# Two thousand columns of an expert's down matrix, moved from the ring into the memory of x

## The chip, the core and the metric

The kernel runs as one program on one core of a Trainium2 chip. The metric is device time in microseconds of one execution; 1854.32 us is the median of three executions of the kernel before (1853.71 to 1855.75).

## What is computed

Two blocks of two layers each work on x, 256 tokens of 1024 numbers, held transposed as eight tiles of 128 x 256. The first block has three kinds of attention and a gated feed-forward part. A layer of the second block, where the change lies, is, cut short:

```
def hybrid_layer(x, ...):
    hn = rms_norm(x, norm_mix)
    ...                                   # attention, latent attention, short convolution
    x = x + einsum('bsc,cd->bsd', mixed, w_out)
    x = x + expert_choice_moe(rms_norm(x, norm_ffn), w_router, b_router, w_gate, w_up, w_down)

def expert_choice_moe(x, ...):            # 16 experts, each takes its 32 best tokens
    gate, idx = lax.top_k(softmax(logits).transpose(0, 2, 1), cap)
    xs = x[bidx, idx]
    hid = silu(xs @ w_gate) * (xs @ w_up)
    return zeros_like(x).at[bidx, idx].add((hid @ w_down) * gate)
```

Each expert has three matrices of 1024 x 1024 fp32 (gate, up, down), 4 MB each. They are read once, so a layer's 16 experts bring 201 MB from HBM.

## The kernel before

**The ring.** All weights stand in HBM as one long stream in the order of use (`ring_plan`, L493). The kernel reads it through a ring in SBUF, 128 partitions x 36096 columns (`RING`, L27; 1024 columns are 512 KB). `layout` (L553) gives each piece a place, one behind the other, and starts again at 0 when a piece doesn't fit. A chunk is one matrix of 8192 columns; `wanted` (L535) says into which pieces it is cut. A piece can be loaded once the instructions that read the older data in the same columns are done.

**Places beside the ring.** Expert 1 (`SPARE`, L31) of each second-block layer gets some pieces elsewhere, written as negative numbers in `wanted`: of its up matrix 2048 columns go into the tile `cst`, six times 512 into the buffers `whi` and `wlo`, four times 256 into `rows_c` and `kb` tiles; of its down matrix eight times 256 go into `kb` tiles. The rest of the down matrix, 2048 and 4096 columns, lies in the ring. `fetch` (L838) makes the tiles and the DMAs.

**The stage around the change.** When x of a layer is complete (x8, eight views of the tile `xT`), the router normalizes it and finds each expert's tokens: a short chain of small steps, with four rounds of `max` and `match_replace` on VectorE (L1731). Meanwhile sixteen transposes bring the normalized x into token order (L1755, four PSUM banks), and eight matmuls with the identity lay x into four PSUM banks, `yj` (L1726); onto these the experts add their outputs, and at the end of the stage x8 is written back from `yj` (L1829). Between these two points nothing reads x8. `gather(0)` (L1768) makes the inputs of experts 0 to 7 with 32 matmuls and eight copies; then expert 0's gate matmuls begin (L1788).

**The order.** No engine runs in program order: `Program.order` (L447) plans all instructions of the whole kernel at once. It schedules forward and backward in turn, `ROUNDS` times, each round ranked by the times of the one before; it keeps the round that its own model finds shortest. The first rank is shaken by random numbers, one seed for each of the four layers (`SEEDS`, L145; entry 2 is the first layer of the second block). An instruction that needs a PSUM bank may be taken early only where the buffers that lie between it and the oldest unissued instruction leave one free (`held`, L368). All DMAs go to SyncE's queue (SP) in the planned order, and a DMA that waits holds up those behind it.

Of the kernel before, what the change touches and what calls it, by code (L numbers as in the profile page):

```python
# [17 lines left out]
T = 256  # L18
# [8 lines left out]
RING, WIDEST = 36096, 4096  # L27
# [107 lines left out]
class Program:  # L135
# [5 lines left out]
    WINDOW, SLACK, MIX = 4000, 0.0, 0.2  # L141
    IN_ORDER = ("whi", "wlo")
    TICK, BUSY = 3413.0, 3060.0
    ROUNDS, PREFER, WAIT = 7, 3000.0, 1.0
    SEEDS, SHAKE = (20, 16, 1, 1), 20.0  # L145
    SWITCH, OTHER = 95.0, {"V": "S", "S": "V"}

    def __init__(self):
# [386 lines left out]
def wanted(tag):  # L535


    kind = tag[0]
    if kind == "early":
        return 2048, 1024, 1024  # L540
    if kind == "eu" and tag[2] == SPARE:
        return (2048, -2048) + (-512,) * 6 + (-256,) * 4
    if kind == "ed" and tag[2] == SPARE:
        return (-256,) * 8 + (2048, WIDEST)
    if kind in ("eg", "eu", "ed") and GATHER < tag[2] < NE - 1:
        return (2 * WIDEST,)
    if kind == "ed" and tag[2] == NE - 1:
        return 4096, 2048, 1024, 1024
    return (WIDEST,)


def layout():

    at, out = 0, []
    for tag in ring_plan():
        cuts, done, pieces, want = cuts_of(tag), 0, [], list(wanted(tag))
        while done < cuts[-1]:
            w = want.pop(0) if len(want) > 1 else want[0]
            if w < 0:
                pieces.append((-w, None))  # L560
                done -= w
                continue
            fits = [c for c in cuts if done < c <= done + min(w, RING - at)]
            if not fits:
                at = 0
                want.insert(0, w)
                continue
            pieces.append((fits[-1] - done, at))
            at += fits[-1] - done
            if fits[-1] - done < min(w, cuts[-1] - done):  # L570
                want.insert(0, w - (fits[-1] - done) if w - (fits[-1] - done) >= 1024 else w)
            done = fits[-1]
        out.append((tag, pieces))
    return out
# [211 lines left out]
def hybrid_kernel(ctx: ExitStack, tc: tile.TileContext, A, out, taps=None):  # L786
    nc = tc.nc
    prog = Program()
    V, S, PE, DMA = (Engine(prog, k, e) for k, e in
                     (("V", nc.vector), ("S", nc.scalar), ("PE", nc.tensor), ("D", nc.sync)))  # L790

    ringp = ctx.enter_context(tc.tile_pool(name="ringp", bufs=1))
    res = ctx.enter_context(tc.tile_pool(name="res", bufs=1))
# [6 lines left out]
    def nm(s):  # L800
        uid[0] += 1
        return f"{s}_{uid[0]}"

    def kb(dt=F32):
        return prog.tile(res, [128, 256], dt, nm("kb"), "kb", 26)
# [6 lines left out]
    def one_of(pool, shape, name, dt=F32):  # L812
        return prog.tile(pool, shape, dt, nm(name), name, 1)
# [8 lines left out]
    ring = ringp.tile([128, RING], F32, name="ring")  # L822
    lying = []

    ahead = []

    def prefetch(others={}):
        tag, pieces = plan[state["at"]]
        ahead.append((tag, fetch(pieces, others)))

    def chunk(*tag):
        if not ahead:
            prefetch()
        got, t = ahead.pop(0)
        assert got == tag, (got, tag)
        return t

    def fetch(pieces, others):  # L838
        state["at"] += 1
        cols, tiles, spare = [0], [], 0  # L840
        for i, (n, at) in enumerate(pieces):
            o = state["off"]
            state["off"] += 128 * n
            before = []
            if at is not None:
                t = View(Slot(lambda at=at, n=n: ring[:, at:at + n], None), [128, n], F32)
                before = [v for a, b, v in lying if a < at + n and b > at]
                lying[:] = [(a, b, v) for a, b, v in lying if not (a >= at and b <= at + n)]
                lying.append((at, at + n, t))
            elif n == 2048:  # L850
                t = one_of(res, [128, 2304], "cst")
            elif n == 512:
                spare += 1
                t = prog.tile(wk, [128, 512], F32, nm("spare"), ("whi", "wlo")[spare % 2], 3)
            elif pieces[i - 1][0] == 512:
                t = one_of(res, [128, 256], "rows_c")
            else:
                t = kb()
            DMA.dma_start(t[:, :n], A["ring"][o:o + 128 * n].rearrange("(p f) -> p f", p=128), after=before)
            for dst, src in others.get(i, ()):  # L860
                DMA.dma_start(dst, src)
            cols.append(cols[-1] + n)
            tiles.append(t)
        return Chunk(cols, tiles)
# [6 lines left out]
    xT = one_of(res, [128, 8, T], "x")  # L871
    x8 = [View(Part(xT, (slice(None), k)), [128, T], F32) for k in range(8)]
# [4 lines left out]
    cst = one_of(res, [128, 2304], "cst")  # L877
# [5 lines left out]
    for q in range(4):  # L883
        prefetch()
        prefetch({0: [(ck, A["ck"]), (cf, A["cf"])]} if q == 2 else {0: [(pv, A["pv"]), (dl, A["dl"])]} if q == 3 else {})
# [179 lines left out]
    for k0, k1, dst in ((0, 4, rows_c[0][:, :512]), (4, 6, rows_c[0][:, 512:]), (6, 8, rows_c[1])):  # L1065
        p = tps()
# [794 lines left out]
```

## Time and profile before

| | |
|---|---|
| median of 3 | 1854.32 us |
| the profiled execution | 1855.18 us |
| its span, first to last instruction | 1853.4 us |
| TensorE matmuls busy | 1485.4 us (80%) |
| VectorE, ScalarE busy | 800.0 us, 649.4 us |
| read from HBM | 591.66 MB |
| granted TensorE clock, mean | 0.903 of full speed |

The 1.8 us between span and time lie outside the instructions. The page's busy time of TensorE is no bound by itself: the stages have different limits, so the page is read by stretches of time, then the waits of a stretch. The two expert stages lie at about 836 to 1265 us and 1419 to 1848 us, the mixers of the second block ahead of each. TensorE's clock has two levels here, granted 1.00 (2.4 GHz) and 0.50 (1.2 GHz).

### The profile page before, as it was taken

What the parts mean: (1) busy time and instruction counts of PE and PEld (TensorE: products, weight loads), DVE (VectorE), ACT (ScalarE), POOL (GpSimd) and SP (SyncE); (2) the same over time, 40 slices, a digit from 0 to 9 for tenths busy, and PEclk for the clock granted to TensorE, in tenths of its full rate; (3) what the DMA queues carried; (4) which work ended last, traced back from release to release, by engine and by line L of the source; (5) the groups of instructions that cost most, each with busy time, mean ns of one, the idle gap of its engine ahead of it and who ended that gap; (6) DMA issues with size and microseconds to landing.
All of it is one profiled execution on the core that took longest, in us unless ns stands there. A gap on an engine that the chain in (4) does not pass through costs nothing.

```text
span 1853.4 us, 34566 instructions
## 1 busy us (share of the span) xinstructions
PE 1485.4 (80%) x14566; PEld 1180.7 (64%) x14566; DVE 800.0 (43%) x2141; ACT 649.4 (35%) x1588; POOL 0.2 (0%) x4
## 2 busy tenths in 40 slices
PE   7999999999999999988566565668998756555655
PEld 6888999888899998875333233337786433333332
DVE  4997769789776786780000000004684000000000
ACT  3865545468554565742000000005762100000001
POOL 0000000000000000000000000000000000000000
PEclk9999999999999999999788878788998888777777
DMA  9979555664454542449999999999456999999997
GB/s 392 426 323 423 209 177 213 254 277 179 167 216 172 199 169 92 165 168 389 429 429 429 430 430 431 429 426 425 165 204 241 431 429 431 430 431 428 430 431 324
DMA packets 44362, 594.93 MB, mean 321 GB/s; under 512 B 5040, under 2 KB 8752, under 8 KB 15536
## 3 DMA queue, kind: packets, MB, share of 16 engines
q1 hardware_dynamic: 44208, 592.73, 77.7%
q8 instruction: 114, 1.87, 0.4%
q14 instruction: 40, 0.33, 0.0%
HBM read 591.66 MB, written 1.05 MB: 320 GB/s over the span
## 4 chain that ended last, share of the span: by engine, by line
PE 51%; DMA 39%; DVE 7%; ACT 1%; issue 1%; SPq 0%; DVEq 0%; ACTq 0%
PE ps L485 41%; DMA ring<-in_ring_dram 39%; PE ps L481 10%; DVE kb L485 3%; ACT kb L485 1%; DVE wlo L485 1%; DVE ring L485 1%; DVE ti L485 1%; DVE h L485 0%; ACT whi L485 0%; DVE x L485 0%; DVE whi L485 0%; SPq L485 0%; DVE aff L485 0%; ACT ti L485 0%
## 5 line engine op out<-in xcount | busy, mean ns | idle before, releaser
L481 PE MATMUL ps<-ring,kb 128*32 128x256 f32 x6016 | 463.2, 475 | 277.1 <-DMA ring<-in_ring_dram 273.3
L481 PEld LDWEIGHTS ps<-ring,kb 128*32 128x32 f32 x6016 | 241.9, 135 | 487.2 <-issue 248.1
L485 PE MATMUL ps<-h,whi 128*128 128x256 f32 x2944 | 436.6, 288 | 9.5 <-DVE h L485 7.6
L485 PEld LDWEIGHTS ps<-h,whi 128*128 128x128 f32 x2944 | 391.7, 194 | 14.6 <-DVE h L485 8.2
L485 DVE TENSOR_TENSOR wlo<-ring,whi 128x512 fp32r<-128x512 f32 (+1 forms) x512 | 335.8, 676 | 96.3 <-ACT whi L485 60.3
L485 DVE TENSOR_TENSOR kb<-kb,ps 128x256 f32<-128x256 f32 x76 | 31.8, 420 | 791.6 <-ACT kb L485 791.3
L485 ACT CAST whi<-ring 128x512 fp32r<-128x512 f32 (+1 forms) x441 | 267.1, 610 | 239.5 <-PE ps L485 212.0
L485 ACT ACTIVATE kb<-ps 32x256 f32<-32x256 f32 (+3 forms) x178 | 66.4, 378 | 571.0 <-PE ps L481 554.3
L485 PE MATMUL ps<-h,wlo 128*128 128x256 f32 x1472 | 247.1, 285 | 0.0
L485 PEld LDWEIGHTS ps<-h,wlo 128*128 128x128 f32 x1472 | 208.8, 193 | 0.3
L485 ACT COPY kb<-ps 128x256 f32<-128x256 f32 (+2 forms) x234 | 78.4, 364 | 287.6 <-PE ps L481 212.4
L485 PE MATMUL ps<-cm,kb 128*128 128x128 f32 (+2 forms) x554 | 85.3, 276 | 49.0 <-DVE kb L485 46.3
L485 PEld LDWEIGHTS ps<-cm,kb 128*128 128x128 f32 (+1 forms) x554 | 68.3, 166 | 74.9 <-DVE kb L485 50.3
L481 PE MATMUL ps<-kb,kb 32*128 32x256 f32 (+6 forms) x1036 | 98.6, 376 | 12.2 <-ACT kb L485 10.1
L485 PE MATMUL ps<-kb,whi 128*128 128x256 f32 x704 | 99.5, 279 | 0.5 <-DVE kb L485 0.4
L481 PEld LDWEIGHTS ps<-kb,kb 32*128 32x128 f32 (+4 forms) x1036 | 67.1, 171 | 36.5 <-ACT kb L485 20.9
L485 PEld LDWEIGHTS ps<-kb,whi 128*128 128x128 f32 x704 | 89.6, 188 | 0.9 <-DVE kb L485 0.9
L485 ACT ACTIVATE kb<-kb,ti 128x256 f32<-128x256 f32 (+1 forms) x161 | 71.2, 462 | 10.8 <-DVE ti L485 10.4
L485 PE MATMUL ps<-kb,wlo 128*128 128x256 f32 x352 | 58.1, 279 | 0.0
L485 DVE TENSOR_TENSOR kb<-kb,kb 128x256 f32<-128x256 f32 (+2 forms) x135 | 55.9, 422 | 3.5 <-ACT kb L485 1.9
L485 PE MATMUL ps<-whi,h 128*128 128x512 f32 (+1 forms) x192 | 55.3, 377 | 0.0
L485 DVE SCALAR_TENSOR_TENSOR kb<-ps,pv,kb 128x255 f32<-128x255 f32 (+2 forms) x102 | 48.3, 480 | 12.5 <-ACT kb L485 11.3
(171 smaller groups left out, 1028.3 us busy)
## 6 DMA issues: line engine op xcount, KB each, us to landing
ring<-in_ring_dram SPq DMA_DIRECT2D x58, 4096.0 KB, 35.1
ring<-in_ring_dram SPq DMA_DIRECT2D x97, 2048.0 KB, 12.2
ring<-in_ring_dram SPq DMA_DIRECT2D x27, 1024.0 KB, 12.4
ring<-in_ring_dram SPq DMA_DIRECT2D x13, 1536.0 KB, 26.3
ring<-in_ring_dram SPq DMA_DIRECT2D x10, 1920.0 KB, 7.7
ring<-in_ring_dram SPq DMA_DIRECT2D x4, 3584.0 KB, 35.4
ring<-in_ring_dram SPq DMA_DIRECT2D x27, 512.0 KB, 16.2
ring<-in_ring_dram SPq DMA_DIRECT2D x4, 3072.0 KB, 36.8
```

The source lines that it names most:

```text
L481: call(*[self.real(a) for a in args], **{k: self.real(v) for k, v in kw.items()})
L485: o.call(*[self.real(a) for a in o.args], **{k: self.real(v) for k, v in o.kw.items()})
```

## The change

The down matrix of expert 1 keeps its eight pieces in `kb` tiles and its last 4096 columns in the ring. Its middle 2048 columns no longer lie in the ring: one DMA of 1024 KB brings them into the tile `xT`, and the chunk's columns of that part are the eight views x8. Because the tile is x's own, this DMA follows the last reader of x8, among them the eight identity matmuls. Each second-block layer then takes 2048 columns less of the ring, and what follows in the ring lies 2048 columns further ahead. Two settings of the planner change with it: six rounds in place of seven, and seed 6 in place of 1 for the first layer of the second block.

```diff
-    ROUNDS, PREFER, WAIT = 7, 3000.0, 1.0
-    SEEDS, SHAKE = (20, 16, 1, 1), 20.0
+    ROUNDS, PREFER, WAIT = 6, 3000.0, 1.0
+    SEEDS, SHAKE = (20, 16, 6, 1), 20.0
@@ def wanted(tag):
     if kind == "ed" and tag[2] == SPARE:
-        return (-256,) * 8 + (2048, WIDEST)
+        return (-256,) * 8 + (-2048, WIDEST)
@@ def prefetch(others={}):
-        ahead.append((tag, fetch(pieces, others)))
+        ahead.append((tag, fetch(tag, pieces, others)))
@@ def fetch(tag, pieces, others):
             elif n == 2048:
-                t = one_of(res, [128, 2304], "cst")
+                t = one_of(res, [128, 2304], "cst") if tag[0] == "eu" else None
 ...
+            if at is None and n == 2048 and tag[0] == "ed":
+                DMA.dma_start(xT, A["ring"][o:o + 128 * n].rearrange("(p k t) -> p k t", p=128, t=T), writes=x8)
+                cols += [cols[-1] + T * (k + 1) for k in range(8)]
+                tiles += x8
+                continue
```

## Rows read from the trace of the kernel before

**Rows 1.** The page, span in 40 slices of 46 us: busy tenths, clock, DMA
```profile
PE   7999999999999999988566565668998756555655
PEclk9999999999999999999788878788998888777777
DMA  9979555664454542449999999999456999999997
GB/s 392 426 323 423 209 177 213 254 277 179 167 216 172 199 169 92 165 168 389 429 429 429 430 430 431 429 426 425 165 204 241 431 429 431 430 431 428 430 431 324
```
**Rows 2.** The chain that ended last: start us, us, what
```profile
836.23 14.02 PE ps L481 x256
...
878.68 38.37 DMA ring<-in_ring_dram
...
1222.90 34.03 DMA ring<-in_ring_dram
...
1419.17 14.02 PE ps L481 x256
...
1819.95 24.56 DMA ring<-in_ring_dram
```
**Rows 3.** Windows: stretch, length, busy us of PE, PEld, DVE, ACT, POOL; clock, DMA share, GB/s
```profile
700.00:725.00 25.00, 23.85 (x180) 21.55 (x178) 16.56 (x33) 13.58 (x31) 0.00 (x0) 1.00 0.30 120
1100.00:1200.00 100.00, 59.10 (x704) 30.45 (x704) 2.72 (x8) 4.91 (x15) 0.00 (x0) 0.78 1.01 431
1350.00:1375.00 25.00, 23.78 (x185) 21.83 (x184) 22.22 (x60) 17.69 (x52) 0.00 (x0) 1.00 0.68 269
```
**Rows 4.** Timeline of SP, the issues before each expert stage: start us, us, issue
```profile
817.64 2.35 SPq L485 DMA_DIRECT2D spare<-in_ring_dram  x5
836.92 3.73 SPq L485 DMA_DIRECT2D ring<-in_ring_dram  x3
...
1399.04 2.73 SPq L485 DMA_DIRECT2D spare<-in_ring_dram  x4
1419.78 20.28 SPq L485 DMA_DIRECT2D ring<-in_ring_dram  x8
```
**Rows 5.** Windows of one and two us around each stage's start (columns as rows 3)
```profile
824.00:826.00 2.00, 0.10 (x1) 0.00 (x0) 1.81 (x7) 1.10 (x4) 0.00 (x0) 1.00 1.05 404
828.00:830.00 2.00, 1.40 (x6) 1.21 (x6) 1.84 (x6) 0.00 (x0) 0.00 (x0) 0.50 0.00 0
836.00:837.00 1.00, 1.00 (x19) 0.58 (x21) 0.42 (x1) 0.98 (x3) 0.00 (x0) 1.00 0.00 0
839.00:840.00 1.00, 1.00 (x24) 0.65 (x20) 0.00 (x0) 0.00 (x0) 0.00 (x0) 1.00 0.97 410
1414.00:1416.00 2.00, 2.00 (x12) 2.00 (x11) 1.89 (x7) 0.75 (x2) 0.00 (x0) 0.50 0.00 0
```
**Rows 6.** Timeline of TensorE across the router: idle before it and releaser in brackets
```profile
820.97 1.94 PE L485 MATMUL ps<-cm,kb 128*128 128x128 f32 x16
823.71 0.39 PE L485 MATMUL ps<-cm,aff 128*16 128x128 f32 x2 [0.80 <-DVE aff L485]
828.09 0.36 PE L485 MATMUL ps<-cm,kb 16*128 16x16 f32 x2 [3.99 <-DVE kb L485]
828.74 0.63 PE L485 MATMUL ps<-sel,ck 128*128 128x32 f32 x2 [0.28 <-DVE sel L485]
830.51 5.73 PE L485 MATMUL ps<-kb,h 128*128 128x256 f32 x32 [0.74 <-DVE kb L485]
836.16 11.43 PE L481 MATMUL ps<-ring,kb 128*32 128x256 f32 x208
...
1412.82 6.35 PE L485 MATMUL ps<-kb,h 128*128 128x256 f32 x32 [0.74 <-DVE kb L485]
```
**Rows 7.** Timeline of TensorE: identity matmuls on x (two records each), projection matmuls
```profile
880.86 1.76 PE L485 MATMUL ps<-x,cm 128*128 128x256 f32 x4
...
905.26 1.03 PE L485 MATMUL ps<-x,cm 128*128 128x256 f32 x4
...
800.78 1.25 PE L485 MATMUL ps<-h,whi 128*128 128x256 f32 x9
```
**Rows 8.** Timeline of VectorE: last write of x, last round, readers of the transposes
```profile
818.04 0.42 DVE L485 TENSOR_TENSOR x<-ps,x 128x256 f32<-128x256 f32 x1
...
827.87 0.46 DVE L485 SCALAR_TENSOR_TENSOR h<-ps,ti,h 128x256 fp32r<-128x256 f32 x1
...
830.71 1.26 DVE L485 SCALAR_TENSOR_TENSOR h<-ps,ti,h 128x256 fp32r<-128x256 f32 x3
```
**Rows 9.** DMA issues: to, from, count, KB each, us from issue to landing
```profile
ring<-in_ring_dram SPq DMA_DIRECT2D x1, 1024.0 KB, 5.1
x<-in_x_dram SPq DMA_DIRECT2D x1, 1024.0 KB, 5.2
```

More of the change, by code (lines that the diff above doesn't have):

```diff
@@ L836, in chunk, with fetch @@
         return t
-    def fetch(pieces, others):
+    def fetch(tag, pieces, others):
         state["at"] += 1
```

## Prediction

> **What bounds the kernel now.** I read the 40 slices first [rows 1]. They split the span in two kinds of stretch. In the mixers TensorE is at 9 tenths and the DMA engines idle half the time; in the two expert stages it is the other way round, the DMA engines at 9 and about 430 GB/s, TensorE at 5 to 6. The windows say the same sharper: 1100 to 1200 us has DMA share 1.01 and 431 GB/s with TensorE busy 59 of 100 us, while 700 to 725 us has TensorE busy 23.85 of 25 us and DMA share 0.30 [rows 3]. The chain of waits agrees: from 836 us to the end it is a burst of TensorE, then DMA pieces of 25 to 38 us joined by short TensorE pieces [rows 2]. So an expert stage ends when its bytes have come: its length is (bytes not yet on chip when the stream becomes saturated) / 430 GB/s, and its end moves with the moment of saturation and with what was loaded before it. Fuller buffers in mid-stage are worth nothing, since the DMA engines never rest there.
>
> The moment of saturation is seen in three views. SP issues its last DMA before the stage at 817.64 us, five in 2.35 us, and the next at 836.92 us [rows 4]. Between them the DMA engines finish what was queued and then stand still: share 1.05 at 824 to 826, 0.00 at 828 to 830 and at 836 to 837, 0.97 from 839 us [rows 5]. TensorE's first expert matmul is at 836.16 us [rows 6], so the issue at 836.92 us is a piece that waited for ring columns which expert 0's gate matmuls read. The second layer repeats it: last spare issues at 1399.04 us, next ring issue 1419.78 us, share 0.00 before it [rows 4, 5]. There are thus some 8 us of idle DMA ahead of each stage, with the ring full. That is what the change can use.
>
> **The change, part by part.**
>
> *The DMA into x.* One DMA of 1024 KB is removed from the ring and one of the same size is added, so no bytes and no issues are added. If it runs in the idle 8 us, the stage has 1.049 MB less to bring: 1.049 MB / 430 GB/s = 2.44 us. The DMA must start after the identity matmuls and land before the stream starts again. Alone, such a DMA lands 5.1 to 5.2 us after its issue [rows 9]; issued by about 831 us it is clear of a restart at 836 to 838 us. If it overlaps the restart a little, its bytes are still moved early, as the engines are not saturated before 839 us.
>
> The Trainium skill states, in "DMA: Bandwidth & Descriptors", Specifications, that HBM gives one core about 358 GB/s. By that the megabyte would be worth 2.93 us. The trace's 430 GB/s disagrees, and decides.
>
> *A later restart.* Ring arithmetic, first layer: expert 0's gate matrix lies at columns 6144 to 14336, and the removed piece at 5120 to 7168. It waited only for the first of the eight groups of gate matmuls (1024 columns each): 836.92 - 836.16 = 0.76 us. After the change the first ring DMA of the stage is the 4096-column piece, now at 5120 to 9216; it must wait for three groups. 208 records in 11.43 us are 0.055 us each [rows 6], a group has eight, so two more groups are 0.88 us. In the second layer everything lies 2048 columns lower, gate 24832 to 33024 and the piece 23552 to 27648: three groups again, against one before. So each layer gains 2.44 - 0.88 = 1.56 us, both 3.1 us, if TensorE's times stay.
>
> *The identity matmuls.* Before, they run deep in the expert stage, at 880.86 us and later, in gaps, where they cost nothing [rows 7]. Now a DMA waits for them, so the planner has a reason to put them ahead of the stage. x is complete at about 818.5 us [rows 8]. A pair of them takes 1.03 us at the full clock (905.26 us) and 1.76 us where most of it ran at the low one (880.86 us) [rows 7]; four pairs make 4.1 to 7.0 us. What can cover that: TensorE's idle stretches in the router, 0.80 + 3.99 + 0.28 + 0.74 = 5.8 us, of which 3.99 us is one piece, while VectorE does the four rounds [rows 6]. In that piece all the matmuls fit at the full clock, nearly. The limit is PSUM: sixteen transposes fill four of eight banks at 820.97 us [rows 6], and VectorE reads the last of them only at 827.87 to 831.97 us [rows 8]. With the router's own bank, three of the four banks for x are free in the gap, so six matmuls (3.1 us) fit there and the last two (1.0 us) fall into the smaller gaps up to 830.5 us. Then nothing on the path is delayed, and the DMA can issue at about 831 us. If the cover is gone, each pair pushes gather and expert 0 back by its 1.03 to 1.76 us.
>
> *The clock.* After the long idle piece the granted clock is 0.50 (1.2 GHz) at 828 to 830 us, and TensorE starts gather in it; the second layer has 0.50 at 1414 to 1416 us [rows 5]. Gather's 32 matmuls take 5.73 and 6.35 us [rows 6]. Matmuls of the same shape at 1.00 are spaced (1.25 - 0.28) / 8 = 0.12 us, taking 0.28 us as the length of one record [rows 7], so 32 of them take about 4.0 us. If the identity matmuls fill the gap and the clock stays at 2.4 GHz, gather ends up to 1.7 and 2.3 us sooner, and the restart with it: 0 to 4.0 us in sum. I take half, 2.0 us, because two of the gaps remain and the eight copies between gather's matmuls may bind first.
>
> *Planner settings.* Seed and round count change no work, but the whole order. In the mixers TensorE idles 1.2 us of 25 (700 to 725, 1350 to 1375 us) [rows 3], so there is little to win or lose in a stage; I take 0 and plus or minus 2 us as an estimate from these two rows. The eight views in place of one, and the write of x8 at the stage's end long after, cost nothing: same matmuls, same columns.
>
> *Sum.* 3.1 + 2.0 = 5.1 us, between 3.1 and 7.1. The profiled execution, 1853.4 us of span in 1855.18 us, would become 1850.1; it lies 0.9 us above the median of the three, so on the median 1854.32 - 5.1 = 1849.2 us, between 1847.2 and 1851.2 without the reordering.
>
> **The rivals.**
>
> *Identity matmuls on the path (slower).* The planner ranks them by the backward pass, where the DMA into x comes just before the first ring piece of the stage; that puts them near gather or between gather and expert 0. There each microsecond of them delays expert 0, and so the restart. All eight cost 4.1 to 7.0 us; with the 0.88 us and less the 2.44 us that is 2.5 to 5.4 us for a layer, 5.1 to 10.9 for both: 1859.4 to 1865.2 us. It decides from 1.56 us of such work per layer, about a pair. For it: PSUM is crowded there [rows 6, 8], and before, the planner left the 3.99 us empty although x was ready. Against it: before, it had no reason to hurry.
>
> *The DMA into x comes too late to matter.* Should the identity matmuls stay behind the start of expert 0, the DMA joins a saturated stream and gains nothing; the later restart is left, 2 x 0.88 us: 1856.1 us. The change then does not do what it says. For it: they stood at 880.86 us before [rows 7]. Against it: SP's order is planned too, and the DMA's place in the stream is early.
> The Trainium skill, "DMA: Bandwidth & Descriptors", Anatomy of one DMA, says that DMA engines don't wait on semaphores; the issuing sequencer waits before dispatch. So a late DMA into x, if placed early on SP, would hold the ring pieces behind it. What this would do here: each microsecond that x's readers end after about 837.8 us delays the restart by as much, so a pair of identity matmuls behind expert 0's first groups adds 1.0 to 1.8 us per layer, 1858 to 1860 us; no row shows such a hold on SP in the gap, and I count it in this rival with 0.04.
>
> *Reordering outweighs it.* If the new order of the four layers is worth more than 2 us either way, 1846 to 1858 us without any help from the change. For it: all stages are planned anew. Against it: the small idle shares [rows 3].
>
> **How the numbers follow.** Forecast 0.55; too late 0.15 (with the 0.04); on the path 0.17; reordering 0.13. Less than 0.2% (3.7 us) is about what a measurement of this kernel can tell from no change; faster means below 1850.6 us. The forecast, with its 2 us of reordering, lies below that in four of five parts: 0.43, and 0.05 from reordering: 0.48. Within 0.2%: the rest of the forecast 0.12, most of "too late" 0.11, partly covered matmuls 0.06, reordering 0.04: 0.33. Slower: 0.19. The range runs from 1847.2 less 2 us of reordering, 1845, to 1856.1 plus 2, 1858; it leaves out the bulk of "on the path" and the ends of reordering, some 0.2.
>
> **What would show it.** In the timeline of TensorE, identity matmuls between 818 and 831 us and gather starting no later than 830.5 us; the granted clock there 1.00 or 0.50. On SP, a DMA into x at about 831 us and the first ring issue some 0.9 us behind the third gate group. In the windows, a DMA share above zero between 828 and 836 us. Each stage's length from expert 0's first matmul to x8's write-back should fall by about 1.6 us, the rest lies ahead of it. Wrong would be: identity matmuls next to gather with expert 0 later by more than 1.6 us, or the DMA into x behind the first ring piece, or a difference that stands in the first 800 us.

## The result: 10.8 us slower, in the mixers

The changed kernel takes 1865.82 us (median of 4, 1864.78 to 1870.17) against 1855.03 us for the kernel before: a ratio of 1.006, 95% interval 1.0048 to 1.0072. The forecast was 1849.2 us and the range ended at 1858; the sign and the range were both wrong. The profiled execution has a span of 1863.6 us in 1865.53 us, 10.2 us more than before. One profiled execution further below, that of the first held run, took 3463.09 us against 1851.03 to 1856.02 us of its ten others; no stage time is taken from it.

The page of the changed kernel, the lines that answer to [rows 1], 40 slices of 46.6 us:

```profile
PE   7999999899999999989566555558999765655655
PEclk9999999999999999989878788888999877878788
DMA  9989555665454541448999999999346999999997
```

The picture is the same: mixers bound by TensorE, expert stages bound by the DMA engines. So the stages have to be timed. I take as marks the last write of x in the first block, then for each second-block layer the start of the last write of x in the mixer and of the first write-back of x from PSUM. The marks of the changed kernel, from the timelines of VectorE and ScalarE (start us, us, instruction):

```profile
824.34 0.42 DVE L485 TENSOR_TENSOR x<-ps,x 128x256 f32<-128x256 f32 x1
...
1269.54 0.92 ACT L485 COPY x<-ps 128x256 f32<-128x256 f32 x3 [1.22 <-PE ps L481]
...
1413.00 0.42 DVE L485 TENSOR_TENSOR x<-ps,x 128x256 f32<-128x256 f32 x1
...
1857.03 1.20 ACT L485 COPY x<-ps 128x256 f32<-128x256 f32 x4 [1.22 <-PE ps L481]
```

In the kernel before the same marks are 818.04 [rows 8], 1264.30, 1400.35 and 1846.86 us. The differences of these marks give the table that carries everything below. Mixer 0 counts from the end of the first block to x complete, experts 0 from there to the write-back, and so on; all in us, from one profiled execution of each kernel; how far a stage moves from one execution to the next was not measured.

| | first block ends | mixer 0 | experts 0 | mixer 1 | experts 1 | span |
|---|---|---|---|---|---|---|
| before | 706.0 | 112.0 | 446.3 | 136.1 | 446.5 | 1853.4 |
| changed | 705.2 | 119.2 | 445.2 | 143.5 | 444.0 | 1863.6 |
| difference | -0.8 | +7.2 | -1.1 | +7.4 | -2.5 | +10.2 |

Both expert stages became shorter, 3.6 us together, as the prediction said. The two mixers became 14.6 us longer, in code that the diff does not touch.

The start of the expert stages in the changed kernel, on SP and TensorE (to be held against [rows 4] and [rows 6]):

```profile
834.32 0.33 SPq L485 DMA_DIRECT2D x<-in_ring_dram  x1
844.77 5.51 SPq L485 DMA_DIRECT2D ring<-in_ring_dram  x4
...
1425.66 0.33 SPq L485 DMA_DIRECT2D x<-in_ring_dram  x1
1432.07 5.53 SPq L485 DMA_DIRECT2D ring<-in_ring_dram  x4
```
```profile
827.99 2.77 PE L485 MATMUL ps<-x,cm 128*128 128x256 f32 x6
...
831.47 0.38 PE L485 MATMUL ps<-cm,aff 128*16 128x128 f32 x2
...
843.21 7.11 PE L481 MATMUL ps<-ring,kb 128*32 128x256 f32 x128
...
1425.03 5.56 PE L485 MATMUL ps<-kb,h 128*128 128x256 f32 x32
1430.52 3.86 PE L481 MATMUL ps<-ring,kb 128*32 128x256 f32 x65
```

The identity matmuls have moved from deep in the stage to the router (827.99 us, before 880.86 [rows 7]), the DMA into x is issued at 834.32 us, and the windows show it filling the idle time and ending before the stage (columns as in rows 3): share 0.98 at 836 to 838 us, then rest. The last line has its 5.0 us from issue to landing.

```profile
836.00:838.00 2.00, 0.97 (x7) 0.78 (x7) 1.91 (x8) 0.00 (x0) 0.00 (x0) 0.92 0.98 393
838.00:840.00 2.00, 2.00 (x10) 2.00 (x11) 2.00 (x8) 0.51 (x2) 0.00 (x0) 0.50 0.17 70
842.00:844.00 2.00, 2.00 (x27) 1.61 (x30) 0.42 (x1) 1.54 (x4) 0.00 (x0) 1.00 0.00 0
...
x<-in_ring_dram SPq DMA_DIRECT2D x1, 1024.0 KB, 5.0
```

The bytes show it directly. From expert 0's first matmul to the write-back of the second layer, 1419.10 to 1846.86 us before and 1430.52 to 1857.03 us in the changed kernel, the DMA engines moved:

```profile
DMA packets 8668, 179.76 MB, mean 420 GB/s; under 512 B 960, under 2 KB 960, under 8 KB 1600
DMA packets 8525, 178.72 MB, mean 419 GB/s; under 512 B 944, under 2 KB 944, under 8 KB 1584
```

That is the megabyte, gone from the stage. So the change does what it says. The question is the mixers.

### The profile page after: what moved, and what is told of

Its sections match the earlier page's. It is cut to its first block, busy times and chain, and to the rows that moved or that the text cites. A ratio compares the mean times of both kernels' runs of the same rounds, so it can differ in the third digit from the quotient of the medians.

```text
span 1863.6 us, 34615 instructions
## 1 busy us (share of the span) xinstructions
PE 1487.9 (80%) x14566; PEld 1179.3 (63%) x14566; DVE 804.0 (43%) x2152; ACT 643.3 (35%) x1577; POOL 0.2 (0%) x4
## 4 chain that ended last, share of the span: by engine, by line
PE 49%; DMA 40%; DVE 8%; ACT 2%; issue 1%; SPq 0%; DVEq 0%; ACTq 0%
DMA ring<-in_ring_dram 40%; PE ps L485 40%; PE ps L481 9%; DVE kb L485 4%; DVE wlo L485 2%; ACT kb L485 1%; DVE ring L485 1%; DVE ti L485 1%; DVE h L485 0%; DVE x L485 0%; ACT whi L485 0%; DVE whi L485 0%; SPq L485 0%; ACT ti L485 0%; DVE sel L485 0%
## 5 line engine op out<-in xcount | busy, mean ns | idle before, releaser
L481 PE MATMUL ps<-ring,kb 128*32 128x256 f32 x5984 | 454.5, 469 | 284.2 <-DMA ring<-in_ring_dram 280.4
L481 PEld LDWEIGHTS ps<-ring,kb 128*32 128x32 f32 x5984 | 235.0, 133 | 490.7 <-issue 238.4
L485 ACT ACTIVATE kb<-ps 32x256 f32<-32x256 f32 (+4 forms) x180 | 66.9, 378 | 600.0 <-PE ps L481 581.0
```

The source lines that it names most:

```text
L481: call(*[self.real(a) for a in args], **{k: self.real(v) for k, v in kw.items()})
L485: o.call(*[self.real(a) for a in o.args], **{k: self.real(v) for k, v in o.kw.items()})
```

## Where the mixers lose it

Two windows at the end of mixer 0, in the changed kernel and then in the kernel before:

```profile
786.00:796.00 10.00, 7.92 (x67) 6.84 (x66) 9.93 (x32) 6.51 (x19) 0.00 (x0) 1.00 0.24 80
796.00:806.00 10.00, 9.25 (x55) 8.96 (x55) 7.22 (x25) 3.59 (x11) 0.00 (x0) 0.66 0.00 0
```
```profile
786.00:796.00 10.00, 9.12 (x73) 7.14 (x71) 9.16 (x33) 7.33 (x24) 0.00 (x0) 1.00 0.31 93
796.00:806.00 10.00, 9.85 (x83) 9.71 (x81) 8.86 (x22) 5.04 (x11) 0.00 (x0) 1.00 0.36 126
```

TensorE waits 1.2 us more in the first ten, and in the second its granted clock is 0.66 on average, with 55 matmuls done where the kernel before did 83. TensorE's own timeline has a wait of 2.08 us for VectorE just ahead of the fall, where the longest wait of the kernel before in this mixer is 0.9 us. Its table of waits for mixer 1 has more and longer ones than before (engine and releaser: us in total, times, longest; two lines of the changed kernel, then one of the kernel before, which has no wait for ScalarE there):

```profile
795.29 1.07 PE L485 MATMUL ps<-cm,kb 128*128 128x1 f32 x8 [2.08 <-DVE kb L485]
```
```profile
PE ps L485 <- DVE kb L485: 6.1, 4, 4.0
PE ps L485 <- ACT kb L485: 2.1, 3, 0.8
```
```profile
PE ps L485 <- DVE kb L485: 4.7, 3, 3.3
```

By the whole-stage windows, mixer 1 lets TensorE rest 143.5 - 132.69 = 10.8 us against 136.0 - 128.79 = 7.2 us before, which is 3.6 us; and its mean clock is 0.95 against 0.97, which over the stage is about 143.5 x 0.05 - 136 x 0.03 = 3.1 us. Together these are most of the 7.4 us. In mixer 0 the mean clock is 0.97 against 1.00, some 3.5 us, and TensorE's idle time grew by 1.0 us. The other 2.7 us fit matmuls that the order moved across the marks: its window has 809 records against 787, and 22 more at the mean of 0.14 us are some 3 us. So these are waits of TensorE, most of them for VectorE, in another order of the same instructions, and a clock of 1.2 GHz for a while behind them. That makes two theories:

- **Order theory.** The planner, given other data and settings, drew another order for the whole kernel, and this order has longer mixers. The new place itself gains what the expert stages show.
- **Place theory.** The DMA into x, and what it does to loads and identity matmuls, slows the mixers by itself.

## The experiments

**Settings alone.** The kernel before, with six rounds and seed 6.

```diff
-    ROUNDS, PREFER, WAIT = 7, 3000.0, 1.0
-    SEEDS, SHAKE = (20, 16, 1, 1), 20.0
+    ROUNDS, PREFER, WAIT = 6, 3000.0, 1.0
+    SEEDS, SHAKE = (20, 16, 6, 1), 20.0
```

> The kernel before with only the planner's settings of the change (six rounds, seed 6); the down matrix stays in the ring. Order theory (the mixers' 14.6 us are lost to a new planned order, the new place itself gains 1.1 and 2.6 us in the two expert stages): expert stages from x complete to x back as before within 0.5 us (446.3 and 446.6), mixers anywhere within 8 us of before, sum 1850 to 1870 us. Place theory (the DMA into x and its identity matmuls slow the mixers): mixers as before within 2 us each, 1853 to 1857 us.

1863.65 us against 1855.27 (ratio 1.0049, interval 1.0034 to 1.0064). An order alone, with no word of the new place, costs 8.4 us. It does so elsewhere than the changed kernel: the first block ends 3.5 us later, mixer 0 takes 110.9 and mixer 1 139.4 us. The expert stages, 447.5 and 447.8 us, are 1.2 and 1.3 us longer, more than the 0.5 us I allowed.

**The place with the old settings.**

```diff
-    ROUNDS, PREFER, WAIT = 6, 3000.0, 1.0
-    SEEDS, SHAKE = (20, 16, 6, 1), 20.0
+    ROUNDS, PREFER, WAIT = 7, 3000.0, 1.0
+    SEEDS, SHAKE = (20, 16, 1, 1), 20.0
```

> The change with the planner's settings of before (seven rounds, seed 1): the new place alone, but under a third order, since the planner plans it anew. Order theory: expert stages 1 to 3 us shorter than before each, mixers within 8 us of before in either direction and not the same as in the changed kernel. Place theory: both mixers again some 7 us longer than before, sum about 1865 us.

1862.66 us (1.0039, 1.0024 to 1.0054). Expert stages 444.0 and 444.1 us, 2.3 and 2.4 us shorter than before. Mixer 0 takes 118.2 us, close to the changed kernel's 119.2, mixer 1 139.8 us. Two kernels with the new place having a mixer 0 of like length spoke for the place theory, though the waits are not the same (here the longest is 1.6 us, for ScalarE, and the clock at 796 to 806 us is 0.83). So the order had to be held fixed.

**The place with the mixers' order held.** The planner gets one more condition, and its result is stored in the kernel as a list (`ORDER`) that `order` returns: an instruction of the mixers or of the first block is taken only when it is the next in the sequence that its engine has in the kernel before.

```diff
                     o = ops[i]
+                    if o.seq is not None and self.nexts[e] != o.seq:
+                        continue
                     t = max(clock[e], o.ready)
```

These two lines belong to the planner that made the list; in the kernel the edit is the list and an `order` that reads it. Where a later run stores another list, its edit is told in words.

The first version left the eight scalings that feed the router free:

> The new place, with every instruction of the mixers and of the first block held to the sequence that each engine has in the kernel before; only the router, the experts and the DMAs are planned. Order theory: mixers as before within 1 us, expert stages 1 to 3 us shorter each, about 1851 us (1849 to 1853). Place theory: mixers again longer by about 7 us each, about 1865 us.

1854.81 us, the median of the ten executions without the profiled one, against 1855.27 (0.9998, 0.9988 to 1.0007). The 10 us are gone, but the 3 us of gain aren't there, nor the 1849 to 1853 us that I expected; why is open, without a stage table for it. The control, planned in the same way with the columns in the ring:

> Control for the run with the new place and the mixers of before: the same way of planning, but the 2048 columns stay in the ring. Both theories: mixers as before within 1 us; 1853 to 1857 us. What it lies above the run with the new place is the price of the place alone, with my 3.1 us from the bytes, plus what the clock gives.

1856.72 us (1.0000, 0.9991 to 1.0009; the ratio is estimated from all executions, and the medians alone would give 1.0008), mixers 112.1 and 136.5, experts 447.1 and 446.0 us. In this control the planner put identity matmuls into the router too, the first at 823.45 us, with the columns still in the ring: the expert stages gained nothing from the matmuls' move alone. The second version holds the eight scalings too:

> The new place with every instruction of the mixers held to the sequence of the kernel before, the eight scalings that feed the router included, which the first run of this kind left free; router, experts and DMAs planned. Order theory: mixers 112 and 136 us as before within 1 us, expert stages (x complete to x back) 1 to 3 us below 446.3 and 446.5, sum 1849 to 1853 us. Place theory: mixers longer, 1855 us and more.

1852.84 us against 1856.03 (0.9981, 0.9971 to 0.9990): faster, by 3.2 us. By operation and tile, TensorE's records between the marks are those of the kernel before, one by one, 786 in mixer 0 and 924 in mixer 1. A control of its own, with the ring and the scalings held, was not run. The marks, from which the table below takes mixers of 112.1 and 137.0 and expert stages of 444.4 and 444.9 us:

```profile
820.29 0.42 DVE L624 TENSOR_TENSOR x<-ps,x 128x256 f32<-128x256 f32 x1
...
1264.68 0.92 ACT L624 COPY x<-ps 128x256 f32<-128x256 f32 x3 [1.22 <-PE ps L620]
```

And the two windows at the end of mixer 0 are those of the kernel before again, with the new place in the kernel:

```profile
786.00:796.00 10.00, 9.12 (x72) 7.22 (x72) 9.86 (x33) 8.55 (x29) 0.00 (x0) 1.00 0.32 93
796.00:806.00 10.00, 9.83 (x83) 9.63 (x82) 8.19 (x24) 4.96 (x12) 0.00 (x0) 1.00 0.14 31
```

**The reverse.** The ring as before, with the mixers held to the changed kernel's sequence, by the same edit.

> The reverse of the held run: the 2048 columns stay in the ring, and every instruction of the mixers and of the first block is held to the sequence that each engine has in the changed kernel; router, experts and DMAs are planned. Order theory: the mixers are about as long as in the changed kernel, 119 and 143 us within 2 us, the expert stages as with the ring, 446 to 448 us, sum 1866 to 1871 us. Place theory: the mixers fall back to 112 and 136 us, about 1856 us.

1876.98 us against 1854.67 (1.0116, 1.0099 to 1.0132). Mixer 0 takes 119.1 us without the new place, as in the changed kernel. TensorE's 808 records there are the changed kernel's, one by one, and the wait and the windows show the same loss:

```profile
796.93 1.07 PE L624 MATMUL ps<-cm,kb 128*128 128x1 f32 x8 [2.07 <-DVE kb L624]
786.00:796.00 10.00, 8.86 (x75) 7.75 (x73) 9.88 (x29) 7.85 (x24) 0.00 (x0) 1.00 0.32 123
796.00:806.00 10.00, 8.31 (x45) 8.05 (x46) 7.46 (x26) 3.09 (x10) 0.00 (x0) 0.66 0.09 28
```

Mixer 1 takes 148.0 us, 4.5 us more than in the changed kernel; it and the sum are outside what I allowed. TensorE rests 13.0 us in it against 10.8, and its 924 matmul records take 2.3 us longer, at a mean clock of 0.93 against 0.95. Only the sequence on each engine is held, not the loads and the router and expert work around it; which of these brings that was not tried. Both directions together settle the main point: the 7.2 us of mixer 0 go with the order and not with the place. For mixer 1 the held run shows the same, 137.0 us with the new place; the reverse shows that it can be long without it, not that its 7.4 us are exactly the order's.

**One more draw on each side.** The changed kernel with seven rounds and seed 8, and the kernel before with seed 8:

```diff
-    ROUNDS, PREFER, WAIT = 6, 3000.0, 1.0
-    SEEDS, SHAKE = (20, 16, 6, 1), 20.0
+    ROUNDS, PREFER, WAIT = 7, 3000.0, 1.0
+    SEEDS, SHAKE = (20, 16, 8, 1), 20.0
```
```diff
-    SEEDS, SHAKE = (20, 16, 1, 1), 20.0
+    SEEDS, SHAKE = (20, 16, 8, 1), 20.0
```

> The changed kernel with seven rounds and seed 8: the same place under one more order. Order theory: expert stages 1 to 3 us shorter than before, mixers differing from those of seed 6 (119.2 and 143.5 us) and of seed 1 (118.2 and 139.8 us) by several us; sum 1850 to 1868 us. Place theory: mixers again some 6 to 7 us longer than before, 1862 to 1866 us.

> The kernel before, ring and all, with seed 8 in place of 1: a new order without the new place. Order theory: expert stages 446 to 448 us as with the other orders that keep the ring, mixers anywhere within 8 us of before, not tied to where the 2048 columns lie; sum 1852 to 1865 us. Against the seed 8 run with the new place, its expert stages should be 2 to 4 us longer each.

With the place 1853.22 us against 1856.03 (0.9983, 0.9974 to 0.9992): faster than the kernel before with nothing held, mixers 111.4 and 134.6, experts 442.3 and 444.0 us. With the ring 1857.58 against 1855.87 (1.0011, 1.0002 to 1.0020), mixers 114.7 and 138.6, experts 446.2 and 446.3 us. With the same seed the new place is thus 3.9 and 2.2 us better in the expert stages.

**The identity matmuls late.** As the held run, with them behind expert 0's first matmuls:

```text
-    matmuls of x by the identity: ahead of gather, where the planner put them
+    matmuls of x by the identity: behind the first matmuls of expert 0
```

> As the first of these, but the identity matmuls stand behind expert 0's first matmuls, so the DMA into x joins the running stream. Bytes theory (only what is loaded in the idle time ahead of the stage counts): no gain from the place and the restart still 0.9 us later, expert stages 0.5 to 1.5 us longer than before each, sum 1855 to 1858 us. If instead the place gained by relieving the ring in mid-stage, the stages would be shorter than before as in the other runs.

1860.10 us against 1856.03 (1.0018, 1.0008 to 1.0027), above the 1855 to 1858 us expected. Expert 0's first matmul is at 835.51 us, the first pair of identity matmuls at 849.85 us, the last from 858.42 us. SP issues the ring first and x at 861.79 us, in the running stream:

```profile
837.08 17.92 SPq L624 DMA_DIRECT2D ring<-in_ring_dram  x5
861.79 0.33 SPq L624 DMA_DIRECT2D x<-in_ring_dram  x1
```

Experts take 447.5 and 450.1 us, 1.2 and 3.6 us longer than before and 3.1 and 5.2 us longer than in the held run. From expert 0's first matmul on, the second layer moves 179.76 MB again, as with the ring; the held run moves 178.71 MB. So what counts is that the megabyte comes in the idle time. The second layer loses more than the 0.5 to 1.5 us I gave. Part of it is SP: in each layer it waits 6.7 us for the identity matmuls with ring pieces behind the DMA into x, and in the second layer the DMA engines come to rest meanwhile, for (2 x 0.31) + (2 x 0.21) = 1.0 us:

```profile
1446.00:1448.00 2.00, 2.00 (x23) 1.32 (x25) 0.42 (x1) 0.00 (x0) 0.00 (x0) 1.00 0.69 295
1448.00:1450.00 2.00, 2.00 (x38) 1.04 (x30) 1.29 (x5) 0.37 (x1) 0.00 (x0) 1.00 0.79 246
```

In the first layer their share stays at 0.93 or more (855 to 880 us). What else the second layer loses is open.

**The wait filled by hand.** As the held run, with TensorE's sequence in the router written out: twelve transposes, affinities, all eight identity matmuls, the last four transposes.

```text
-    transposes of hn 1 to 16 and the matmuls of x as planned
+    transposes 1 to 12 | transposes of aff | matmuls of x 1 to 8 | transposes 13 to 16
```

> As the run before, but TensorE's sequence in the router is set by hand: all eight identity matmuls behind the two transposes of the affinities, in the long wait for the four rounds, with four of the sixteen transposes of the normalized x moved behind them so that four PSUM banks are free. If the clock stays at 2.4 GHz when the wait is filled, gather takes about 4.0 instead of 5.7 to 6.4 us, expert 0 begins 1 to 2 us sooner and the expert stages are 2.5 to 3.9 us below before: 1848 to 1851 us. Rival: the moved transposes hold gather up by their own chain through ScalarE and VectorE; then expert 0 begins as late as before and the stages gain 1.6 us at most.

1852.18 us (0.9981, 0.9971 to 0.9990), as good as the held run and no better beyond the noise, and short of the 1848 to 1851 us expected. The two layers differ. In the second the clock stays at 1.00 through the wait where it was 0.50 before (1408 to 1410 us; in [rows 5] still at 1414 to 1416 us), and gather, here with four more matmuls, takes 4.52 us against 6.35 [rows 6]; expert 0 begins 17.2 us after x, 1.5 us sooner than before. The wait in the kernel before, then here:

```profile
1408.00:1410.00 2.00, 0.00 (x0) 0.00 (x0) 1.86 (x7) 0.00 (x0) 0.00 (x0) 0.50 1.03 387
```
```profile
1408.00:1410.00 2.00, 2.00 (x12) 1.77 (x11) 1.81 (x7) 0.50 (x2) 0.00 (x0) 1.00 0.97 396
```
```profile
1414.82 4.52 PE L624 MATMUL ps<-kb,h 128*128 128x256 f32 x36 [0.83 <-DVE kb L624]
1419.28 11.43 PE L620 MATMUL ps<-ring,kb 128*32 128x256 f32 x208
```

In the first the identity matmuls fill the wait too and the clock is 1.00 through it, but it falls at about 833.1 us, half a microsecond into gather, after waits of 1.20 and 0.74 us, and gather takes 6.00 us; expert 0 begins 18.8 us after x, 0.7 us later than before:

```profile
825.61 3.62 PE L624 MATMUL ps<-x,cm 128*128 128x256 f32 x16
829.06 0.97 PE L624 MATMUL ps<-cm,kb 128*128 128x128 f32 x6
831.24 0.41 PE L624 MATMUL ps<-sel,ck 128*128 128x32 f32 x2 [1.20 <-DVE sel L624]
831.48 0.38 PE L624 MATMUL ps<-sel,cm 128*128 128x16 f32 x2
832.59 6.00 PE L624 MATMUL ps<-kb,h 128*128 128x256 f32 x36 [0.74 <-DVE kb L624]
```

**Both together.** Seed 8's mixers held, and the router by hand:

```text
-    mixers in the sequence of the kernel before
+    mixers in the sequence of the seed 8 run
```

> The new place with the mixers held to the sequence of the seed 8 run and TensorE's router sequence set by hand as in the run with the filled wait. If the two gains add: expert stages 2.5 to 4 us below before each, mixers 111 and 135 us, 1848 to 1852 us; if the filled wait gives nothing beyond what the seed 8 order had (expert 0 begins 16.0 and 17.7 us after x there, before any hand), about 1853 us as there.

1856.06 us against 1855.87 (1.0004, 0.9995 to 1.0013). That is neither of the two times expected. The gains don't add: expert stages 443.7 and 443.4 us, 0.8 us more in sum than seed 8's own, and mixer 1 back at 136.7 us. In the first layer the seed 8 order already has its affinities' transposes 5.4 us after x and expert 0 at 16.0 us; that this leaves nothing for the filled wait to win is likely, not shown.

All profiled executions but that of the first held run, in us. The kernel before, run beside each of them, has medians of 1854.67 to 1856.03 us, so the medians here compare to about 1 us.

| columns in | order | median | mixer 0 | experts 0 | mixer 1 | experts 1 |
|---|---|---|---|---|---|---|
| ring | before | 1855.03 | 112.0 | 446.3 | 136.1 | 446.5 |
| ring | settings of the change | 1863.65 | 110.9 | 447.5 | 139.4 | 447.8 |
| ring | before, replanned | 1856.72 | 112.1 | 447.1 | 136.5 | 446.0 |
| ring | seed 8 | 1857.58 | 114.7 | 446.2 | 138.6 | 446.3 |
| ring | changed mixers | 1876.98 | 119.1 | 448.0 | 148.0 | 448.5 |
| x | changed | 1865.82 | 119.2 | 445.2 | 143.5 | 444.0 |
| x | old settings | 1862.66 | 118.2 | 444.0 | 139.8 | 444.1 |
| x | before, held | 1852.84 | 112.1 | 444.4 | 137.0 | 444.9 |
| x | before, wait filled | 1852.18 | 112.1 | 445.0 | 137.3 | 443.4 |
| x | seed 8 | 1853.22 | 111.4 | 442.3 | 134.6 | 444.0 |
| x | seed 8, wait filled | 1856.06 | 112.0 | 443.7 | 136.7 | 443.4 |
| x, late | before, held | 1860.10 | 112.1 | 447.5 | 137.3 | 450.1 |

Expert stages: 446.0 to 448.5 us in ten with the ring, 442.3 to 445.2 us in twelve with x early. The two groups do not overlap. In the second layer, from expert 0's first matmul on, the five with the ring and the late one move 179.76 to 179.77 MB, the six with x early 178.71 to 178.72 MB.

## Why the prediction was wrong, step by step

**The bytes.** Right. The megabyte lands 5.0 us after its issue in the idle time, and the DMA engines rest again before the stage.

**The later restart.** Right in mechanism and size. From expert 0's first matmul to the first ring issue it was 0.76 us in the first layer [rows 4, 6] and 1419.78 - 1419.10 = 0.68 us in the second; now it is 844.77 - 843.21 = 1.56 and 1432.07 - 1430.52 = 1.55 us. Two groups of gate matmuls were put at 0.88 us and cost 0.80 and 0.87.

**The identity matmuls.** Half right. They went into the router, as forecast, though not only because a DMA waits for them: two of the five orders with the ring have some there as well. And the rival that puts them between gather and expert 0 did not come as such: in the first layer they all end before gather. But there they did cost: VectorE had the affinities ready 5.6 us after x as before, but matmuls of x stood ahead of their transposes, at the low clock, and these came 831.47 - 824.34 = 7.1 us after x against 5.7 us before; 0.75 us of it reached expert 0. The step had counted only the long wait and the gaps behind it, not the one ahead. In the second layer expert 0 came 1.2 us sooner, although four records ran into gather (1424.14 to 1425.03 us).

**The clock.** Gather took 5.53 and 5.56 us against 5.73 and 6.35, where 4.0 was the bound for a clock that stays up: of 4.0 us possible, 1.0 came. The half that I took, 2.0 us, was too much. The run with the wait filled shows the full mechanism in one layer and its absence in the other.

**The sum of the expert stages.** First layer 2.44 - 0.80 - 0.75 = 0.9 us, measured 1.1; second 2.44 - 0.87 + 1.23 = 2.8 us, measured 2.5. So 3.6 us of the 5.1 forecast, and inside the bounds of 3.1 to 7.1. From expert 0's first matmul to the write-back the stages fell by 1.8 and 1.3 us, where the prediction had 1.6 each.

**Planner settings.** This is the step that failed. It said that seed and rounds "change no work, but the whole order", and then took 0 with plus or minus 2 us, from TensorE's idle time in the mixers [rows 3]. The 2 us do not follow from those rows: 1.2 us of 25 is 12 us over the 248 us of the two mixers. And that share bounds what a better order can win; it says nothing of what a worse one can lose. A worse order adds waits that the trace of before doesn't have, and stretches at 1.2 GHz come on top, here 3.5 and 3.1 us. The two mixers measured +14.6 us, seven times the bound, and the settings alone cost 8.4 us without the place. The rival "reordering outweighs it" had the right mechanism with 0.13 and an end at 1858 us; it deserved more chance and another 10 us of range. And the order depended not on the settings only: with the old settings the new place was planned anew too, and came out at 1862.66 us.

**The other rivals.** "Too late to matter" was priced at 1856.1 us, from 0.88 us per layer, and at 1858 to 1860 us where the late DMA holds up SP, with 0.04; made on purpose it took 1860.1 us, and SP was held, 6.7 us per layer, though behind five ring pieces and not at the restart. "On the path" was not met.

What stays open is whether the new place also tilts the planner towards long mixers. Three orders drawn with it have mixer 0 at 119.2, 118.2 and 111.4 us, three with the ring at 112.0, 110.9 and 114.7 us. Three each can't tell a tilt from luck; that mixer 0's time goes with the order, whatever drew it, is shown by the two held runs.

## What to carry to other kernels

Where one planner orders the whole kernel, a local edit is also a new draw for all the rest: hold the untouched stages to their old sequence, price the edit there, and only then look for a good draw; here the edit is worth some 3 us of 1855 in the held run and the draws differ by some 10. Ahead of a stage that is bound by transfers, look for the time in which the DMA engines rest because their memory is full: memory that is dead then is worth at most its bytes divided by the rate, less what the next loads wait longer (here 2.44 us less 0.8 to 0.9). Idle time in a stage bounds a gain and not a loss.

## What was not expected of the chip

One wait of 2.08 us in TensorE's sequence at the end of mixer 0 came just before a stretch of 1.2 GHz: clock 1.00 on average at 786 to 796 us and 0.66 at 796 to 806, where 55 matmuls were done instead of 83. And the clock fell while TensorE showed hardly any idle time: in the router of the changed kernel's first layer it was busy 3.94 of the 4 us from 824 to 828 us, with small matmuls among the work (128x1 and 128*32 in the rows), and stood at 0.50 at 828 to 830 us.

```profile
823.99 1.09 PE L485 MATMUL ps<-cm,kb 128*128 128x1 f32 x8
825.01 1.07 PE L485 MATMUL ps<-kb,pv 128*32 128x256 f32 x16
...
824.00:826.00 2.00, 2.00 (x26) 1.34 (x24) 1.11 (x3) 0.57 (x2) 0.00 (x0) 1.00 0.99 406
826.00:828.00 2.00, 1.94 (x18) 1.84 (x15) 0.77 (x5) 0.84 (x3) 0.00 (x0) 0.86 0.97 391
828.00:830.00 2.00, 2.00 (x6) 1.62 (x6) 1.66 (x9) 0.95 (x3) 0.00 (x0) 0.50 0.96 393
```

In the kernel before the fall came behind an idle stretch [rows 5, 6].
